# Transposing attention probabilities and keys by block transfers and VectorE instead of TensorE, in a hybrid decoder layer

## The chip, the cores and the metric

The kernel runs on one core of a Trainium2 chip. The metric is the device time of one execution in microseconds (us), as the median of several runs. Five engines matter here: TensorE (PE in the profile, its weight loads PEld), VectorE (DVE), ScalarE (ACT), GpSimd (POOL) and SyncE (SP), whose queue issues nearly all transfers. Each engine executes its own list of instructions in order and waits at semaphores for the others.

## The reference

One decoder layer on x of 2048 tokens by 1024 features, float32:

- RMSNorm, then one projection to 2816 columns that feeds two groups of heads.
- Four HGRN2 heads (128 wide): a gate f in (0, 1), k = 1 - f, state S_t = diag(f_t) S_{t-1} + k_t v_t^T, output S_t^T q_t, computed in chunks, then normed per head and multiplied by silu of a gate projection.
- Eight attention heads of 64 on two key/value heads, with a sliding window of 128 tokens and a learned sink logit per head that joins the softmax's denominator: each block of 128 queries sees its own and the previous block of 128 keys.
- Both groups together go through the output projection and are added to x; then RMSNorm, a gated MLP of 2816 with a causal depthwise convolution of three taps on the gate, a residual sum, and a last RMSNorm.

```python
p = jnp.exp(scores - m)
denom = jnp.sum(p, axis=-1, keepdims=True) + jnp.exp(sink - m)
out = jnp.einsum('bnhgqk,bnkhd->bnqhgd', p / denom, vb)
```

The sum over keys in the last line wants the probabilities with the keys on the partitions, while the softmax leaves them with the queries there. In the HGRN2 chunks, k v^T wants the keys' tokens on the partitions, while the projection leaves the features there. These are the two places where the kernel transposes and where the change is made.

## The kernel before, in words

Activations lie feature-major: a tile has 128 features on its partitions and 1024 tokens (HALF) in its rows. The sequence is worked in two halves, and each half runs through three stages: a mix stage (HGRN2 heads and attention), then the output projection with the gate/up products, then the down projection. Every float32 product of weights is three matmuls of a high and a low part (unit, L203 to L219).

In the mix stage (L1105 to L1127) the table ORDER names the pieces of four HGRN2 heads (hgrn: f, q, l, s, p) and four pairs of attention heads (attend: qa, sc, and twice pv or pw) in the order in which they are written. A scheduler with a timeline of its own then sets the final order of every engine's list, so that a change of an operation can shift instructions far away from it.

The pieces that the change touches:

- `sc` (L378 to L427): for each group g of four blocks of 128 queries, the scores are computed (psc, L399), copied to the tile sc, which holds 2 x 4 squares of 128 queries x 128 keys. A masked copy (L408) puts the own block's scores over the previous block's where the key is not after the query: as the window is as long as a block, each square holds every key once, the own block's in one triangle and the previous block's in the other. Then come the maximum (L411), eight exponentials on ACT (L421) and the division by the denominator (L426).
- `pv`, `pw` (L429 to L458): for each g, eight squares of sc are transposed by TensorE against the identity into PSUM (ppt, L435), VectorE multiplies each by two masks into po and pp (L438), and TensorE multiplies them with the values (poT, L446).
- `l` (L474 to L553): seven levels, m = 1 to 64. At each, TensorE makes plev (L517, L531) from K and Q, and VectorE multiplies K and Q by a factor (L523, L524, L534, L535) for the next level; plev is copied into ST by a masked copy (L542) or by ACT. The next level's matmuls wait for that level's Q or K.
- `s` (L555 to L579): K of the last level is transposed by TensorE in squares (pkn, L564), copied by ACT to Kn (L565) and multiplied with v (pu, L571).
- the carry (L345 to L347, L364 to L366): the last block of keys and values of the first half is kept for the second, by two VectorE copies each way.
- The output projection's first units are pop (L682, issued at L218); their operands XH and XL are splits of the finished heads (L225 to L234), and they stand partly among the last head's levels.

Weights come through `prep` (L192 to L201): a transfer on the SP queue into one of three raw tiles, an ACT cast and a VectorE difference.

Of the kernel before, what the change touches and what calls it, by code (L numbers as in the profile page):

```python
# [8 lines left out]
F32 = mybir.dt.float32  # L9
F32R = mybir.dt.float32r  # L10
U32 = mybir.dt.uint32
I32 = mybir.dt.int32
AF = mybir.ActivationFunctionType
ALU = mybir.AluOpType
# [3 lines left out]
P = 128  # L18
# [3 lines left out]
HALF = 1024  # L22
NH = S // HALF
TT = HALF // P
NB = HALF // 512
HG = 4
# [23 lines left out]
def hymba_layer(ctx: ExitStack, tc: tile.TileContext, a: dict, out: bass.AP, rows_out: bass.AP):  # L50
    nc = tc.nc
# [6 lines left out]
    cp = pool("const")  # L58
# [4 lines left out]
    dp = pool("dram", space=bass.MemoryType.DRAM)  # L63
# [5 lines left out]
    def ps(kind, name):  # L69
        return spaces[kind].tile([P, 512], F32, tag=kind, name=name)  # L70
# [6 lines left out]

    nmw = cp.tile([P, 16], F32, name="nmw")[:, 0:KT]
    nc.scalar.dma_start(nmw, a["norm_mix_w"])
    ones = cp.tile([P, P], F32, name="ones")  # L80
    nc.vector.memset(ones, 1.0)
    ident = cp.tile([P, P], F32, name="ident")
    state = cp.tile([P, HG, P], F32, name="state")
    warm = cp.tile([P, 32], F32, name="warm")[:, 0:1]
    nc.scalar.activation(warm, ones[:, 0:1], AF.Tanh)
    nc.gpsimd.memset(ident, 1.0)
    nc.gpsimd.affine_select(out=ident, in_=ident, compare_op=ALU.is_equal, fill=0.0,
                            base=0, pattern=[[-1, P]], channel_multiplier=1)
    halo = cp.tile([P, FT, 2], F32, name="halo")
    nc.vector.memset(halo, 0.0)  # L90
    kc = cp.tile([P, 2, P], F32R, name="kcarry")
    vc = cp.tile([P, P], F32, name="vcarry")

    class C:
        pass
# [3 lines left out]
    def constants():  # L99

        C.own = cp.tile([P, P], F32, name="own")
        C.ownT = cp.tile([P, P], F32, name="ownT")
        C.prevT = cp.tile([P, P], F32, name="prevT")
        for t, op, sgn in ((C.own, ALU.is_ge, 1), (C.ownT, ALU.is_ge, -1), (C.prevT, ALU.is_gt, 1)):
            nc.gpsimd.memset(t, 1.0)
            nc.gpsimd.affine_select(out=t, in_=t, compare_op=op, fill=0.0, base=0,
                                    pattern=[[-sgn, P]], channel_multiplier=sgn)

        C.lmask = {}
        for m in LEVELS[:5]:  # L110
            t = cp.tile([P, 2, 64], F32, name=f"lmask{m}")
            nb = 64 // m
            nc.gpsimd.memset(t, 1.0)
            for side in range(2):
                ts = t[:, side]
                nc.gpsimd.affine_select(out=ts, in_=ts, compare_op=ALU.is_ge, fill=0.0, base=-side * m,
                                        pattern=[[-2 * m, nb], [0, m]], channel_multiplier=1)
                nc.gpsimd.affine_select(out=ts, in_=ts, compare_op=ALU.is_ge, fill=0.0, base=m - 1 + side * m,
                                        pattern=[[2 * m, nb], [0, m]], channel_multiplier=-1)
            C.lmask[m] = t  # L120

        battn = C.battn = cp.tile([P, 6], F32, name="battn")
        nc.sync.dma_start(battn, a["b_attn"])
        C.bq = cp.tile([P, ATT_J], F32, name="bq")
        nc.vector.tensor_scalar(C.bq, battn[:, 0:ATT_J], 0.125, None, op0=ALU.mult)
        C.hgw = cp.tile([P, 1], F32, name="hgw")
        nc.sync.dma_start(C.hgw, a["hg_norm_w"])
        nc.vector.tensor_scalar(C.hgw, C.hgw, 0.5, None, op0=ALU.mult)
        C.sinkb = cp.tile([P, ATT_J, 2], F32, name="sinkb")
        nc.sync.dma_start(C.sinkb.rearrange("p j k -> p (j k)"), a["sinks"].to_broadcast([P, 8]))  # L130
        C.nfw = cp.tile([P, KT], F32, name="nfw")
        nc.sync.dma_start(C.nfw, a["norm_ffn_w"])
        C.fnw = cp.tile([P, KT], F32, name="fnw")
        nc.sync.dma_start(C.fnw, a["final_norm_w"])
        C.cw = cp.tile([P, FT, 4], F32, name="cw")
        nc.sync.dma_start(C.cw, a["conv"])

        lbl = cp.tile([P, 2, HG], F32, name="lbl")
        nc.sync.dma_start(lbl, a["lb_logits"])
        lbm = cp.tile([P, HG], F32, name="lbm")  # L140
        nc.vector.tensor_tensor(lbm, lbl[:, 0], lbl[:, 1], op=ALU.max)
        lbe = cp.tile([P, 2, HG], F32, name="lbe")
        nc.vector.tensor_tensor(lbe, lbl, lbm.unsqueeze(1).to_broadcast([P, 2, HG]), op=ALU.subtract)
        nc.scalar.activation(lbe, lbe, AF.Exp)
        nc.vector.tensor_tensor(lbm, lbe[:, 0], lbe[:, 1], op=ALU.add)
        nc.vector.reciprocal(lbm, lbm)
        C.lb = cp.tile([P, HG], F32, name="lb")
        nc.vector.tensor_tensor(C.lb, lbe[:, 0], lbm, op=ALU.mult)
        C.omlb = cp.tile([P, HG], F32, name="omlb")
        nc.vector.tensor_scalar(C.omlb, C.lb, -0.5, 0.5, op0=ALU.mult, op1=ALU.add)  # L150
        nc.vector.tensor_scalar(C.lb, C.lb, 0.5, 0.5, op0=ALU.mult, op1=ALU.add)
# [178 lines left out]
    def across(t, base, dims):  # L330

        v = t[:, :]
        return bass.AP(v.tensor, v.offset + base, [list(v.ap[0])] + dims)

    def rows(kv):
        return slice(kv * HD, (kv + 1) * HD)

    def att_keys(hf, kv, invb, p):
# [4 lines left out]
        KS = p.tile([P, 2, P + HALF], F32R, name="KS")  # L343
        V = p.tile([P, 1 + TT, P], F32, name="V")
        if hf:  # L345
            nc.vector.tensor_copy(KS[:, :, 0:P], kc)
            nc.vector.tensor_copy(V[:, 0], vc)  # L347
        kT, vT = [p.tile([P, HALF], F32, tag="f", name=n, bufs=2) for n in ("kT", "vT")]
        for jj, dst in ((ATT_J, kT), (ATT_J + 1, vT)):
            o = kv[jj - ATT_J]  # L350
# [11 lines left out]
                nc.tensor.transpose(pv[:, i * P:(i + 1) * P], vT[:, t0:t0 + P], ident)  # L362
            nc.scalar.copy(V[:, 1 + 4 * b:5 + 4 * b].rearrange("p a b -> p (a b)"), pv)
        if hf + 1 < NH:  # L364
            nc.vector.tensor_copy(kc, KS[:, :, HALF:HALF + P])
            nc.vector.tensor_copy(vc, V[:, TT])  # L366
        return KS, V

    def attend(hf, j, X, invb, KS, V, mix, p):
# [7 lines left out]
        yield  # L377
        scs = []  # L378
        for g in range(NB):
            sc = p.tile([P, 2, 4, P], F32, tag="sc", name="sc", bufs=2)  # L380
            gs = slice(g * 512, (g + 1) * 512)
            for kv in range(2):
                r, other = rows(kv), rows(1 - kv)
# [43 lines left out]
            scs.append(sc)  # L427
        yield
        for g, sc in enumerate(scs):  # L429
            pm = []  # L430
            for kv in range(2):
                pm.append([p.tile([P, 4, P], F32, tag="pp", name=n, bufs=4) for n in ("po", "pp")])
                pt = ps("at", "ppt")
                for i in range(4):
                    nc.tensor.transpose(pt[:, i * P:(i + 1) * P], sc[:, kv, i], ident)  # L435
                ptv = pt.rearrange("p (i q) -> p i q", i=4)
                for dst, mk in zip(pm[kv], (C.ownT, C.prevT)):
                    nc.vector.tensor_tensor(dst, ptv, mk.unsqueeze(1).to_broadcast([P, 4, P]), op=ALU.mult)  # L438
            oT = ps("at", "poT")
            for i in range(4):  # L440
                n = g * 4 + i
# [18 lines left out]
    def hgrn(hf, h, X, invb, vs, WG, gates, mix, p, fu=None):  # L460
# [95 lines left out]

        kept = TT if hf + 1 < NH else TT - 1
        Kn = p.tile([P, TT, P], F32, tag="t4", name="Kn", bufs=2)
        for b in range(NB):
            pk = ps("hg", "pkn")  # L560
            n = min(4, kept - 4 * b)
            for i in range(n):
                c = slice((b * 4 + i) * P, (b * 4 + i + 1) * P)
                nc.tensor.transpose(pk[:, i * P:(i + 1) * P], K[:, c], ident)  # L564
            nc.scalar.copy(Kn[:, 4 * b:4 * b + n].rearrange("p a b -> p (a b)"), pk[:, 0:n * P])  # L565
# [636 lines left out]
```

## Time and profile before

| | |
|---|---|
| median of 3 runs | 2150.81 us (2150.37 to 2150.9) |
| span of the profiled execution | 2149.0 us |
| the median above that span | 1.8 us |
| PE busy | 2130.8 us, 99% |
| PEld busy | 1790.6 us, 83% |
| DVE busy | 1632.2 us, 76% |
| ACT busy | 1020.2 us, 47% |
| transfers | 35.6% of 16 engines' span, 254.41 MB |

The page gives the span from the first to the last instruction of one execution; the runs' times lie 1.8 us above it. A busy share is an average over unlike stages. The mix stages lie at about 60 to 390 us and 1125 to 1450 us of the span, the gate/up and down stages between and after them. A matmul's row has a duration that is pipelined with the next one: what an instruction costs its engine is read from the distance between starts in the timeline, not from the duration.

### The profile page before, as it was taken

The page shows a single profiled execution, that of the slowest core. Times are in us where ns is not written, and L with a number is a line of the kernel's source. Part 1 is how long each engine was busy: PE and PEld are TensorE (multiplying, and loading weights), DVE is VectorE, ACT ScalarE, POOL GpSimd, SP SyncE. Part 2 cuts the span into 40 slices and gives each one's busy share as a digit, 9 for nine tenths or more (in the row PEclk, how much of TensorE's full clock was granted, in tenths as well). Part 3 has the DMA queues.
Part 4 walks back from the last instruction along what each step waited for, and adds up shares of the span by engine and source line. Part 5 has one row for each costly group of instructions (what it writes and reads, how often), then busy time and mean ns, then how long its engine had stood idle before and what let it go on. Part 6 is the DMA issues. An engine that isn't in the chain of part 4 may idle for free.

```text
span 2149.0 us, 29228 instructions
## 1 busy us (share of the span) xinstructions
PE 2130.8 (99%) x11271; PEld 1790.6 (83%) x11271; DVE 1632.2 (76%) x2443; ACT 1020.2 (47%) x1818; POOL 16.2 (1%) x45
## 2 busy tenths in 40 slices
PE   8999999999999999999999999999999999999998
PEld 6988988888888888888889889888888888888887
DVE  6576768788887888785775767677988888787765
ACT  5445554564444445345634446535544444443453
POOL 2000000000000000000000000000000000000000
PEclk9999999999999999999999999999999999999999
DMA  4111012413332334974641111124223323359743
GB/s 158 40 30 40 31 30 79 137 62 125 94 122 89 103 118 147 371 255 145 217 138 40 30 31 33 40 75 158 69 104 103 118 84 122 95 187 398 236 147 133
DMA packets 91147, 254.41 MB, mean 118 GB/s; under 512 B 11136, under 2 KB 13952, under 8 KB 91008
## 3 DMA queue, kind: packets, MB, share of 16 engines
q1 hardware_dynamic: 90576, 252.29, 35.3%
q8 instruction: 88, 1.44, 0.3%
q14 instruction: 51, 0.42, 0.1%
q10 hardware_dynamic: 432, 0.27, 0.0%
HBM read 195.37 MB, written 57.15 MB: 118 GB/s over the span
## 4 chain that ended last, share of the span: by engine, by line
PE 93%; DVE 5%; ACT 1%; issue 1%; DMA 0%; SPq 0%; DVEq 0%; ACTq 0%
PE X L767 7%; PE X L766 7%; PE X L765 7%; PE pop L218 6%; PE q L218 4%; PE f L218 4%; PE hq L218 4%; PE Y L767 4%; PE Y L765 4%; PE Y L766 4%; PE pdx L954 3%; PE pdx L953 3%; PE pdx L952 3%; PE g L218 3%; PE pdy L953 3%; PE pdy L954 3%
## 5 line engine op out<-in xcount | busy, mean ns | idle before, releaser
L638 ACT CAST whi<-raw 128x1024 fp32r<-128x1024 f32 x88 | 92.7, 1053 | 115.5 <-PE X L766 71.1
L765 PE MATMUL X<-T,whi 128*128 128x512 f32 x352 | 136.9, 389 | 0.0
L766 PE MATMUL X<-T,whi 128*128 128x512 f32 x352 | 136.9, 389 | 0.0
L767 PE MATMUL X<-T,wlo 128*128 128x512 f32 x352 | 136.9, 389 | 0.0
L836 DVE SCALAR_TENSOR_TENSOR y<-ga,cw,y 128x1024 f32<-128x1024 f32 x88 | 112.7, 1280 | 25.9 <-ACT y L834 25.8
L639 DVE TENSOR_TENSOR wlo<-raw,whi 128x1024 fp32r<-128x1024 f32 x88 | 107.3, 1219 | 4.4 <-ACT whi L638 4.4
L771 ACT COPY u<-X 128x512 f32<-128x512 f32 x88 | 51.6, 586 | 122.5 <-PE X L767 122.2
L199 ACT CAST whi<-raw 128x1024 fp32r<-128x1024 f32 x58 | 60.5, 1048 | 98.8 <-issue 20.6
L639 DVE TENSOR_TENSOR xld<-raw,xhd 128x1024 fp32r<-128x1024 f32 x72 | 81.1, 1132 | 17.8 <-ACT xhd L638 17.6
L638 ACT CAST xhd<-raw 128x1024 fp32r<-128x1024 f32 x72 | 69.8, 978 | 39.1 <-DMA raw<-act0T 14.0
L218 PE MATMUL pop<-XL,whi 128*128 128x512 f32 x256 | 84.2, 392 | 0.9 <-DVE XL L230 0.9
L218 PE MATMUL pop<-XH,wlo 128*128 128x512 f32 x256 | 83.3, 391 | 0.8 <-DVE wlo L200 0.8
L218 PE MATMUL pop<-XH,whi 128*128 128x512 f32 x256 | 83.1, 396 | 0.8 <-ACT XH L229 0.5
L200 DVE TENSOR_TENSOR wlo<-raw,whi 128x1024 fp32r<-128x1024 f32 x58 | 70.5, 1220 | 9.8 <-ACT whi L199 9.8
L767 PEld LDWEIGHTS X<-T,wlo 128*128 128x128 f32 x352 | 66.1, 188 | 13.7
L766 PEld LDWEIGHTS X<-T,whi 128*128 128x128 f32 x352 | 66.1, 188 | 13.7
L765 PEld LDWEIGHTS X<-T,whi 128*128 128x128 f32 x352 | 66.0, 188 | 13.7
L630 PE MATMUL pvv<-whi,XH 128*128 128x256 f32 x256 | 73.0, 286 | 0.0
L631 PE MATMUL pvv<-whi,XL 128*128 128x256 f32 x256 | 72.9, 286 | 0.0
L632 PE MATMUL pvv<-wlo,XH 128*128 128x256 f32 x256 | 71.9, 285 | 0.0
L767 PE MATMUL X<-B,wlo 128*128 128x512 f32 x176 | 68.7, 390 | 0.7 <-DVE wlo L639 0.7
L765 PE MATMUL X<-T,Sh 128*128 128x512 f32 x176 | 68.7, 390 | 0.0
(390 smaller groups left out, 6399.2 us busy)
## 6 DMA issues: line engine op xcount, KB each, us to landing
wr<-in_w_down SPq DMA_DIRECT2D x90, 512.0 KB, 5.6
raw<-in_w_gate SPq DMA_DIRECT2D x44, 512.0 KB, 3.6
raw<-in_w_up SPq DMA_DIRECT2D x44, 512.0 KB, 3.6
raw<-act0T SPq DMA_DIRECT2D x20, 512.0 KB, 5.9
raw<-act1T SPq DMA_DIRECT2D x20, 512.0 KB, 5.6
act0B<-y SPq DMA_DIRECT2D x33, 256.0 KB, 2.3
act1B<-y SPq DMA_DIRECT2D x33, 256.0 KB, 2.4
raw<-in_w_out SPq DMA_DIRECT2D x16, 512.0 KB, 3.7
```

The lines of the kernel that those rows point to most:

```text
L218: nc.tensor.matmul(o[b], w, x[:, bs], start=f, stop=l)
L630: nc.tensor.matmul(o[:, 0:256], xh[:, t], hi[:, c], start=kt == 0, stop=False)
L631: nc.tensor.matmul(o[:, 0:256], xl[:, t], hi[:, c], start=False, stop=False)
L632: nc.tensor.matmul(o[:, 0:256], xh[:, t], lo[:, c], start=False, stop=kt == KT - 1)
L638: nc.scalar.copy(h, src)
L639: return (eng or nc.vector).tensor_tensor(l, src, h.bitcast(F32), op=ALU.subtract)
L765: nc.tensor.matmul(o, wh[:, ws], xh, start=i == 0 and not more, stop=False, skip_group_check=more)
L766: nc.tensor.matmul(o, wh[:, ws], xl, start=False, stop=False, skip_group_check=more)
L767: nc.tensor.matmul(o, wl[:, ws], xh, start=False, stop=i == 3, skip_group_check=more)
L836: nc.vector.scalar_tensor_tensor(y, g[:, w:w + HALF], C.cw[:, ft, w:w + 1], y, op0=ALU.mult, op1=ALU.add)
L953: nc.tensor.matmul(o, wh[:, i, c], al[:, i, cols], start=False, stop=False, skip_group_check=more)
L954: nc.tensor.matmul(o, wl[:, i, c], ah[:, i, cols], start=False, stop=l, skip_group_check=more)
```

## The change

Four things change together.

- The eight squares of sc per group are no longer transposed by TensorE. A new helper `moved` issues 16 transfers on the SP queue; each takes a block of 32 partitions x 8 squares x 32 columns and puts it where the transposed square has that block, in runs of 32 floats (128 bytes). A second helper `turned` lets VectorE transpose every 32x32 block of the result in place of rows (one instruction for 128x1024). The results are md and pt, and they share the buffers of sc, of which there are now three instead of two.
- po is still pt times the mask ownT; pp is now pt minus po instead of pt times prevT.
- For heads 0 to 2, K is transposed to Kn by the same two helpers (over a tile Kd). Head 3 keeps TensorE's transposes.
- The carry goes through two small tiles in DRAM by four transfers; the tiles ones and prevT are gone.

```diff
-    kc = cp.tile([P, 2, P], F32R, name="kcarry")
-    vc = cp.tile([P, P], F32, name="vcarry")
+    kc = dp.tile([P, 2, P], F32, name="kcarry")
+    vc = dp.tile([P, P], F32, name="vcarry")
...
+    def moved(dst, src):
+
+        for a in range(4):
+            for c in range(4):
+                nc.sync.dma_start(dst[32 * c:32 * c + 32, :, 32 * a:32 * a + 32],
+                                  src[32 * a:32 * a + 32, :, 32 * c:32 * c + 32])
+
+    def turned(dst, src):
+
+        nc.vector.transpose(dst.rearrange("p a b -> p (a b)"), src.rearrange("p a b -> p (a b)"))
...
-            nc.vector.tensor_copy(KS[:, :, 0:P], kc)
-            nc.vector.tensor_copy(V[:, 0], vc)
+            nc.sync.dma_start(KS.bitcast(F32)[:, :, 0:P], kc)
+            nc.sync.dma_start(V[:, 0], vc)
...
-            sc = p.tile([P, 2, 4, P], F32, tag="sc", name="sc", bufs=2)
+            sc = p.tile([P, 2, 4, P], F32, tag="sc", name="sc", bufs=3)
...
         for g, sc in enumerate(scs):
+            md, pt = [p.tile([P, 8, P], F32, tag="sc", name=n, bufs=3) for n in ("md", "pt")]
+            moved(md, sc.rearrange("p a b c -> p (a b) c"))
+            turned(pt, md)
             pm = []
             for kv in range(2):
                 pm.append([p.tile([P, 4, P], F32, tag="pp", name=n, bufs=4) for n in ("po", "pp")])
-                pt = ps("at", "ppt")
-                for i in range(4):
-                    nc.tensor.transpose(pt[:, i * P:(i + 1) * P], sc[:, kv, i], ident)
-                ptv = pt.rearrange("p (i q) -> p i q", i=4)
-                for dst, mk in zip(pm[kv], (C.ownT, C.prevT)):
-                    nc.vector.tensor_tensor(dst, ptv, mk.unsqueeze(1).to_broadcast([P, 4, P]), op=ALU.mult)
+                ptv = pt[:, 4 * kv:4 * kv + 4]
+                own, prv = pm[kv]
+                nc.vector.tensor_tensor(own, ptv, C.ownT.unsqueeze(1).to_broadcast([P, 4, P]), op=ALU.mult)
+                nc.vector.tensor_tensor(prv, ptv, own, op=ALU.subtract)
...
         Kn = p.tile([P, TT, P], F32, tag="t4", name="Kn", bufs=2)
-        for b in range(NB):
+        if h < HG - 1:
+            Kd = p.tile([P, TT, P], F32, tag="SS", name="Kd", bufs=1)
+            moved(Kd, K.rearrange("p (c t) -> p c t", t=P))
+            turned(Kn, Kd)
+        for b in range(NB if h == HG - 1 else 0):
             pk = ps("hg", "pkn")
```

The scheduler makes a new order of the whole mix stage from this. Three places matter for what follows. The first is TensorE's list at the end of the first half's mix stage, in the levels of head 3 (pop is the output projection, ppt a transposed square, psc the scores, poT the product with the values). Before, around the matmuls of the level m = 4:

```order
L218 MATMUL pop_3548<-XH,wlo 128x512
L218 MATMUL pop_3549<-XH,wlo 128x512
L517 MATMUL plev<-Q,G 128x2x64 x4
L435 MATMUL ppt<-ident,sc 128x128 x4
L218 MATMUL pop_3623<-XH,whi 128x512
L218 MATMUL pop_3623<-XL,whi 128x512
```

And now, at the end of 24 pop matmuls:

```order
L216 MATMUL pop_3710<-XL,whi 128x512
L216 MATMUL pop_3710<-XH,wlo 128x512
L527 MATMUL plev<-Q,G 128x2x64 x16
L541 MATMUL plev<-Q,K 32x32 x16
L541 MATMUL plev<-Q,K 64x64 x8
L456 MATMUL poT<-po,V 64x128 x2
L578 MATMUL pkn<-ident,K 128x128 x8
L456 MATMUL poT<-pp,V 64x128 x2
```

Before, four matmuls of a level stand between long rows of pop (and of g and psc); now four levels (x16), the two coarse ones and pkn follow each other with two poT between. The pop matmuls that stood there are behind pu now. The second half's list has the same piece, with four psc after the level m = 2 and x12 after them.

The second place is VectorE's list beside it. Before, up to the factors of the level m = 2, for which the matmuls of m = 4 wait (XL is a split for the output projection, wlo a weight's low part, sc the masked copy of scores, hg the gate's product):

```order
L523 TENSOR_TENSOR K<-K,F_3003 128x2x128x2
L408 COPY_PREDICATED sc<-own,psc 128x256
L230 TENSOR_TENSOR XL<-hg_538,XH 128x1024
L230 TENSOR_TENSOR XL<-att_1697,XH 128x1024
L200 TENSOR_TENSOR wlo<-raw,whi 128x1024
L504 SCALAR_TENSOR_TENSOR hg_2104<-sg,hg_2104 128x512 x2
L230 TENSOR_TENSOR XL<-att_1508,XH 128x1024
L523 TENSOR_TENSOR K<-K,F_3015 128x2x64x4
L524 TENSOR_TENSOR Q<-Q,F_3003 128x2x128x2
```

Now, up to the same factors, and the later stretch in which the block transpose stands:

```order
L533 TENSOR_TENSOR K<-K,F_3071 128x2x128x2
L434 RECIPROCAL den<-den 128x8
L514 SCALAR_TENSOR_TENSOR hg_2139<-sg,hg_2139 128x512
L420 TENSOR_REDUCE m<-sc 128x8
L514 SCALAR_TENSOR_TENSOR hg_2139<-sg,hg_2139 128x512
L435 TENSOR_TENSOR sc<-sc,den 128x1024
L514 SCALAR_TENSOR_TENSOR hg_3033<-sg,hg_3033 128x512 x2
L533 TENSOR_TENSOR K<-K,F_3083 128x2x64x4
L423 TENSOR_TENSOR m<-m,sinkb 128x8
L534 TENSOR_TENSOR Q<-Q,F_3071 128x2x128x2
```

```order
L435 TENSOR_TENSOR sc<-sc,den 128x1024
L534 TENSOR_TENSOR Q<-Q,F_3107 128x2x16x16
L552 COPY_PREDICATED ST<-lmask_309,plev 128x2x16x16
L342 STREAM_TRANSPOSE pt<-md 128x1024
L544 TENSOR_TENSOR Q<-Q,F_3119 128x16x32
L545 TENSOR_TENSOR K<-K,F_3119 128x16x32
L447 TENSOR_TENSOR po<-pt,ownT 128x512
L448 TENSOR_TENSOR pp<-pt,po 128x512
L447 TENSOR_TENSOR po<-pt,ownT 128x512
L544 TENSOR_TENSOR Q<-Q,F_3141 128x8x64
L545 TENSOR_TENSOR K<-K,F_3141 128x8x64
```

The softmax of attention pair 3 stands among the levels now where splits and weight parts stood, and the block transpose and its masks stand ahead of the last two levels' factors.

The last place is the SP queue early in the first half. Before, weights alone stood there; now, in one piece (Kd and md are the targets of `moved`, 16 transfers each):

```order
L196 DMA raw<-in_w_f 128x1024
L374 DMA kcarry<-KS 256x1x128
L375 DMA vcarry<-V 128x128
L196 DMA raw<-in_w_g 128x1024
L196 DMA raw<-in_w_q 128x1024
L337 DMA Kd<-K 32x8x32 x16
L196 DMA raw<-in_w_att 128x1024 x2
L196 DMA raw<-in_w_g 128x1024
L337 DMA md<-sc 32x8x32 x16
L196 DMA raw<-in_w_f 128x1024
```

The transfers of blocks stand in the same queue as the weights, and a transfer that waits for its tile holds back the weights behind it.

More of the change, by code (lines that the diff above doesn't have):

```diff
@@ L79, in hymba_layer @@
     nc.scalar.dma_start(nmw, a["norm_mix_w"])
-    ones = cp.tile([P, P], F32, name="ones")
-    nc.vector.memset(ones, 1.0)
     ident = cp.tile([P, P], F32, name="ident")
@@ L84, in hymba_layer @@
     warm = cp.tile([P, 32], F32, name="warm")[:, 0:1]
-    nc.scalar.activation(warm, ones[:, 0:1], AF.Tanh)
+    nc.vector.memset(warm, 1.0)
+    nc.scalar.activation(warm, warm, AF.Tanh)
     nc.gpsimd.memset(ident, 1.0)
@@ L102, in constants @@
         C.ownT = cp.tile([P, P], F32, name="ownT")
-        C.prevT = cp.tile([P, P], F32, name="prevT")
-        for t, op, sgn in ((C.own, ALU.is_ge, 1), (C.ownT, ALU.is_ge, -1), (C.prevT, ALU.is_gt, 1)):
+        for t, op, sgn in ((C.own, ALU.is_ge, 1), (C.ownT, ALU.is_ge, -1)):
             nc.gpsimd.memset(t, 1.0)
@@ L364, in att_keys @@
         if hf + 1 < NH:
-            nc.vector.tensor_copy(kc, KS[:, :, HALF:HALF + P])
-            nc.vector.tensor_copy(vc, V[:, TT])
+            nc.sync.dma_start(kc, KS.bitcast(F32)[:, :, HALF:HALF + P])
+            nc.sync.dma_start(vc, V[:, TT])
         return KS, V
```

## The prediction

> **What bounds the kernel now.** I read the page first, then the busy time of single stretches, then the timelines at the places that the new order changes.
>
> ```profile
> span 2149.0 us, 29228 instructions
> PE 2130.8 (99%) x11271; PEld 1790.6 (83%) x11271; DVE 1632.2 (76%) x2443; ACT 1020.2 (47%) x1818; POOL 16.2 (1%) x45
> PEclk9999999999999999999999999999999999999999
> PE 93%; DVE 5%; ACT 1%; issue 1%; DMA 0%; SPq 0%; DVEq 0%; ACTq 0%
> ```
>
> TensorE works for 2130.8 of 2149.0 us, at full clock, and is 93% of the chain of waits: what leaves its list is won, as long as nothing makes it wait. VectorE's 76% is an average. The windows show its share at the end of the mix stages, where the change adds work to it (columns: stretch, length, PE, PEld, DVE, ACT, POOL, granted clock, DMA share, GB/s):
>
> ```profile
> core 0: us, PE busy (x) PEld busy (x) DVE busy (x) ACT busy (x) POOL busy (x), PEclk, DMA share, GB/s
> 320.00:340.00 20.00, 20.00 (x133) 16.97 (x132) 19.81 (x28) 11.47 (x19) 0.00 (x0) 1.00 0.49 154
> 340.00:372.00 32.00, 30.64 (x256) 25.29 (x256) 23.14 (x43) 12.35 (x45) 0.00 (x0) 1.00 0.13 37
> 1400.00:1430.00 30.00, 28.56 (x225) 23.34 (x226) 25.86 (x44) 9.45 (x29) 0.00 (x0) 1.00 0.28 96
> ```
>
> At 320 to 340 us both engines are full, 19.81 and 20.00 of 20: TensorE never waits although VectorE is saturated, because pop matmuls stand between the levels. In the two later stretches TensorE idles 32 - 30.64 = 1.4 and 30 - 28.56 = 1.4 us, 2.8 together.
>
> **What is removed.** All 128 transposes of probabilities go, and 45 of the 60 of keys (head 3 keeps 8 + 7): 173. Their price is the distance between starts, with the neighbours' own cost taken off (start, duration, instruction, count):
>
> ```profile
> L435 PE MATMUL ppt<-ident,sc 128*128 128x128 f32 x128 | 18.0, 273 | 0.0
> L564 PE MATMUL pkn<-ident,K x60: 270/272/301, 97.9 to 1427.0; 128*128 128x128 f32 x60
> 137.40 0.60 PE L435 MATMUL ppt<-ident,sc 128*128 128x128 f32 x4
> 137.76 0.70 PE L218 MATMUL q<-XH,wlo 128*128 128x512 f32 x2
> 138.29 0.63 PE L218 MATMUL q<-XH,whi 128*128 128x512 f32 x2
> 138.76 0.62 PE L218 MATMUL q<-XL,whi 128*128 128x512 f32 x2
> ```
>
> Two q take 138.76 - 138.29 = 0.47 us. The four transposes and two q before them take 138.29 - 137.40 = 0.89, so four transposes 0.42: 0.105 each. I take 0.11, so 173 x 0.11 = 19.0 us. The group's 18.0 busy us over 128 give 0.14 and 24.2 us as the upper end. [...]
>
> ACT loses twelve copies of pkn; nothing waits there, so I count them at zero, with TensorE's stream as cover. VectorE loses the four carry copies.
>
> **What is added.** VectorE gets 22 block transposes of 128x1024. No row shows one. The nearest rows are its other operations of that size (1.13 us, below); bounds are half and twice that, 0.6 to 2.3, and I take 1.13. The subtraction for pp costs what the product with prevT cost. SP gets 22 moves of 16 transfers and four carry transfers:
>
> ```profile
> 1.23 0.90 SPq L312 DMA_DIRECT2D x<-in_xP  x2
> 1390.53 0.33 SPq L198 DMA_DIRECT2D raw<-in_w_out  x1
> out<-h SPq DMA_DIRECT2D x12, 64.0 KB, 1.7
> ```
>
> Issued back to back a transfer costs 0.90 / 2 = 0.45 us of the queue, alone 0.33; the smallest frequent one lands after 1.7. A move is then 16 x 0.45 + 1.7 = 8.9 us; the ends are 7.0 (0.33 each) and 16.1 (0.9 each, twice the row, because one transfer is 256 runs of 128 bytes, which no row has). In the middle of the stage a move is covered: between a group's last exponentials and its poT stand rows of 512-column matmuls, 71 of them (16 us at 0.235) for the first pair. A weight queued behind a move is up to 8.9 us late; three raw tiles lie ahead of it, and I count nothing. The carry's reader stands a half later: nothing.
>
> **The order is what decides.** In the new lists the levels m = 2 to 16 of head 3, the two coarse levels and pkn follow each other with no pop between. TensorE then waits for VectorE's factors, so this stretch lasts as long as VectorE's list there. Prices on VectorE from these rows, start to start:
>
> ```profile
> 320.61 0.20 DVE L425 RECIPROCAL den<-den 128x8 f32<-128x8 f32 x1
> ...
> 327.50 1.32 DVE L542 COPY_PREDICATED ST<-lmask,plev 128x512 f32<-128x512 uint32 x1
> 328.61 1.26 DVE L230 TENSOR_TENSOR XL<-hg,XH 128x1024 fp32r<-128x1024 f32 x1
> ...
> 330.72 1.21 DVE L230 TENSOR_TENSOR XL<-hg,XH 128x1024 fp32r<-128x1024 f32 x1
> 331.86 1.21 DVE L230 TENSOR_TENSOR XL<-att,XH 128x1024 fp32r<-128x1024 f32 x1
> ...
> 345.01 0.70 DVE L542 COPY_PREDICATED ST<-lmask,plev 128x512 f32<-128x512 uint32 x1
> 345.61 0.68 DVE L504 SCALAR_TENSOR_TENSOR hg<-sg,hg 128x512 f32<-128x512 f32 x1
> 346.21 0.68 DVE L438 TENSOR_TENSOR po<-ppt,ownT 128x512 f32<-128x512 f32 x1
> ```
>
> 1.14 us for 1024 columns, 0.60 for 512, a masked copy 1.1 in the first levels and 0.60 later, 0.20 at most for 8 columns (0.12 taken; all at 0.20 would add 0.6). From the first factor (K by f, m = 1) to the last, K by F_3141, VectorE's list of the first half holds 22 operations of 512 columns (13.2 us), five masked copies (2 x 1.1 + 3 x 0.6 = 4.0), four of 1024 columns with the transpose (4.5), two masked copies of 256 columns (0.7) and seven small ones (0.8): 23.2 us.
>
> TensorE's work beside it, from its timeline:
>
> ```profile
> 339.27 1.05 PE L517 MATMUL plev<-Q,G 128*128 128x128 f32 x8
> 340.15 0.60 PE L435 MATMUL ppt<-ident,sc 128*128 128x128 f32 x4
> ...
> 351.85 0.70 PE L531 MATMUL plev<-Q,K 128*32 128x32 f32 x32
> ...
> 358.84 0.69 PE L531 MATMUL plev<-Q,K 128*64 128x64 f32 x16
> ```
>
> 24 pop at 0.235 (5.6), 8 psc (about 1.0), four levels at 340.15 - 339.27 = 0.88 (3.5), then the coarse levels' 0.70 and 0.69: 11.5 us. It waits 23.2 - 11.5 = 11.7, plus about 1 us that VectorE comes late behind pdiag: 13. In the second half VectorE's list holds 23.5 us, and den there waits for eight exponentials issued within the stretch:
>
> ```profile
> 121.38 0.39 ACT L421 ACTIVATE sc<-sc,m 128x128 f32<-128x128 f32 x1
> ...
> 124.62 0.19 ACT L421 ACTIVATION_READ_ACCUMULATOR sc<-sc,m 128x1 f32 x1
> ```
>
> They take 124.62 + 0.19 - 121.38 = 3.4 us, of which some 2.5 are not covered by the one factor, masked copy and small operations that stand ahead: 26, and about 27 with the late start, against 11 us of TensorE's work: 16. Together 29 us of waits where 2.8 stood: 26.
>
> Two smaller terms. In the second half pair 3's last block transpose stands nine operations of 512 columns (5.4 us) behind the division that its move waits for, and the move takes 8.9: VectorE stops 3.5 us, and the split XL of hg behind it, for which pop waits, is late by about 2.5. And the clock: after an idle start, TensorE ran slowly for some microseconds.
>
> ```profile
> 5.85 1.42 PE L218 MATMUL kv<-XH,whi 128*128 128x512 f32 x2 [5.85 <-ACT XH L232]
> 7.06 0.63 PE L218 MATMUL kv<-XL,whi 128*128 128x512 f32 x1
> 7.49 0.63 PE L218 MATMUL kv<-XH,wlo 128*128 128x512 f32 x1
> ```
>
> Starts 0.43 apart against 0.235 per q later. The waits in the new stretches are 2 to 3 us each with 0.9 us of work between. If the grant falls there, the levels' slower matmuls still lie inside the waits; the pop behind would run slowly for about 4 us, 2 us lost per half. Bounds 0 and 14 (all that stands there at half speed besides); I take 2. [...]
>
> **The sum.** -19.0 + 26 + 2.5 + 2 = +11.5: 2149.0 + 11.5 = 2160.5, and with the 1.8 us by which the runs' median lies above the span, about 2162.5. By the transpose at 0.14 it is 2157; by a block transpose of 0.6 or 2.3 us, one or two of which lie in each tail, some 1.5 us less or 4 more; by a clock term of 14, 2174. The forecast's own range is 2155 to 2175.
>
> **Rivals.** *Moves slower than their room* (slower, 2188). At 0.9 us per transfer a move takes 16.1. The first move of pair 3 has 10.6 us of VectorE's list ahead of its transpose in the tail, which it then exceeds by 5.5; the second one is 7.2 later than summed. Over two halves 2 x (5.5 + 7.2) = 25 more. It decides from about (10.6 - 1.7) / 16 = 0.56 us per transfer. For it: 256 runs of 128 bytes, and weights share the queue. Against it: the 0.33 of the lone transfers. [...]
>
> *The tails wait half as long* (faster, 2145 to 2146). If VectorE reaches the first factor with its splits and hg products already done, or its list runs beside TensorE's psc and pop better than summed, the extra waits come to some 13, with no late split (0) and a clock term of 0: -19 + 13 = -6, so 2145. It decides where the waits added are below 19. For it: 1.4 us of idle time was all that these stretches had before. Against it: at 320 to 340 us VectorE is already full, so it can't come early.
>
> *The wait is given back* (about 2152, no change). VectorE and the weights catch up while TensorE stands, and what idle time lies elsewhere (2149.0 - 2130.8 = 18.2, of which 5.9 lie ahead of the first matmul and 2.8 in the tails) shrinks by up to its remaining 9.5: 2162.5 - 9.5 = 2153. Against it: most of these waits are for the first inputs of a stage, not for a late engine.
>
> *A transpose costs TensorE its whole duration* (faster, 2134): 173 x 0.273 = 47 in place of 19. Against it: the starts above.
>
> **How the numbers follow.** Forecast 0.58, slow moves 0.19, half the waits 0.10, given back 0.11, the whole duration 0.02. The likeliest gives 2162.5. The range reaches from 2147, below the no-change case, to 2188, the slow moves. What a measurement can tell from no change is about 0.2%, 4.3 us: faster is below 2146.5, slower above 2155.1. Faster is half the waits and the whole duration, 0.12; no change is the given-back case, 0.11; slower is the rest, 0.77.
>
> **What would show it.** In the profile after: TensorE's busy time about 19 us lower; its idle time in the last 30 us of both mix stages about 14 each, put down to VectorE's Q and K (L534, L544, L545); the block transpose near 1.1 us; Kd and md transfers 0.45 apart on the queue; the clock dipping there or not. It is wrong if plev waits for less than half of that, if VectorE is seen idle ahead of the block transposes in the tails (then the moves decide), or if TensorE's waits lie in the middle of the mix stages, behind Kn, poT or weights, where I counted none.

## The result, and the profile after

| | before | after |
|---|---|---|
| median of the runs | 2150.59 us | 2172.88 us |
| ratio to before, 95% interval | | 1.0104 (1.009 to 1.0119) |
| span of the profiled execution | 2149.0 us | 2170.8 us |
| mean granted clock of TensorE | 0.999 | 0.988 |

The change makes the kernel 22.3 us slower. The forecast was 2162.5 us, 12 slower, with a range to 2188: sign and range hold, the size is half of what was measured. Two executions that took over three times as long as the others, 7016.05 us in the variant tail_two_queues and 7636.4 us in the kernel before, are left out of all times here. The page of the changed kernel (first rows, and the clock in 40 slices):

```profile
span 2170.8 us, 29356 instructions
PE 2128.5 (98%) x11098; PEld 1786.2 (82%) x11098; DVE 1655.6 (76%) x2461; ACT 1015.0 (47%) x1806; POOL 19.4 (1%) x43
PEclk9999998999999999999999999979999999999999
```

TensorE idles 2170.8 - 2128.5 = 42.3 us where it was 2149.0 - 2130.8 = 18.2: 24.1 more. And its busy time is only 2.3 us lower, although 173 instructions are gone. The slices with an 8 and a 7 in the clock's row are the ends of the two mix stages. The windows that were shown for the kernel before, and one more (stretch, length, PE, PEld, DVE, ACT, POOL, clock, DMA share, GB/s):

```profile
320.00:340.00 20.00, 17.99 (x130) 15.59 (x128) 18.52 (x33) 12.54 (x36) 0.00 (x0) 1.00 0.37 123
340.00:372.00 32.00, 22.93 (x162) 19.32 (x164) 24.15 (x44) 8.89 (x29) 0.00 (x0) 0.68 0.26 50
1400.00:1430.00 30.00, 19.29 (x165) 16.81 (x163) 26.93 (x49) 15.03 (x52) 0.00 (x0) 0.72 0.18 40
1430.00:1460.00 30.00, 25.55 (x164) 21.57 (x165) 11.72 (x29) 6.39 (x22) 0.00 (x0) 0.82 0.18 42
```

Nearly all of the loss stands here: TensorE is idle for 26.2 us of these 112, and the granted clock is down to 0.68. What TensorE waits for is read in its timeline, first half (start, duration, instruction, count, idle ahead of it and what ended it), with one row of the second half at the end:

```profile
336.92 1.07 PE L527 MATMUL plev<-Q,G 128*128 128x128 f32 x8
342.50 2.04 PE L527 MATMUL plev<-Q,G 128*128 128x128 f32 x8 [4.51 <-ACT G L525]
345.42 2.04 PE L527 MATMUL plev<-Q,G 128*128 128x128 f32 x8 [0.88 <-DVE Q L534]
348.34 2.05 PE L527 MATMUL plev<-Q,G 128*128 128x128 f32 x8 [0.87 <-DVE Q L534]
351.17 1.07 PE L541 MATMUL plev<-Q,K 128*32 128x32 f32 x32 [0.78 <-DVE Q L534]
354.95 1.12 PE L541 MATMUL plev<-Q,K 128*64 128x64 f32 x16 [2.71 <-DVE K L545]
...
358.08 1.94 PE L578 MATMUL pkn<-ident,K 128*128 128x128 f32 x8 [0.60 <-DVE K L545]
...
1414.00 2.04 PE L527 MATMUL plev<-Q,G 128*128 128x128 f32 x8 [3.04 <-ACT G L525]
```

The levels of head 3 wait for VectorE's Q and K, and for G, ACT's copy of that K. After the first long wait the same eight matmuls take 2.04 us instead of 1.07. The granted clock there is half of full speed in three stretches (the third one follows a wait of 2.94 us for the split XL):

```profile
341.40:361.90 20.50, 12.84 (x102) 11.05 (x104) 15.02 (x26) 7.17 (x25) 0.00 (x0) 0.50 0.25 41
1413.20:1437.10 23.90, 13.94 (x112) 12.22 (x113) 16.19 (x28) 7.38 (x26) 0.00 (x0) 0.50 0.25 42
1443.90:1447.40 3.50, 3.50 (x10) 2.73 (x9) 2.89 (x8) 0.00 (x0) 0.00 (x0) 0.51 0.56 206
```

TensorE works for 12.84 + 13.94 + 3.50 = 30.3 us at half clock, so an estimated 15.1 us of its busy time are due to the clock. Without them its work is 2.3 + 15.1 = 17.4 us less than before. The span's growth is then complete: 24.1 more idle + 15.1 - 17.4 = 21.8 us. The rows of VectorE beside it, some of the factors and a block transpose:

```profile
331.89 0.69 DVE L533 TENSOR_TENSOR K<-K,f 128x512 f32<-128x512 f32 x1
344.58 0.69 DVE L534 TENSOR_TENSOR Q<-Q,F 128x512 f32<-128x512 f32 x1 [0.40 <-PE plev L527]
347.50 0.69 DVE L534 TENSOR_TENSOR Q<-Q,F 128x512 f32<-128x512 f32 x1 [0.79 <-PE plev L527]
352.39 1.25 DVE L342 STREAM_TRANSPOSE pt<-md 128x1024 f32<-128x1024 f32 x1 [0.65 <-issue]
357.26 0.68 DVE L545 TENSOR_TENSOR K<-K,F 128x512 f32<-128x512 f32 x1
```

From the first factor to the last, 357.94 - 331.89 = 26.1 us pass. VectorE now also waits for TensorE: its factor changes Q in place and must let the slow plev read Q first (0.40, 0.79). In the kernel before, the same stretch was not shorter but longer, and TensorE had more pop to do in it:

```profile
323.56 0.69 DVE L523 TENSOR_TENSOR K<-K,f 128x512 f32<-128x512 f32 x1
360.19 0.69 DVE L535 TENSOR_TENSOR K<-K,F 128x512 f32<-128x512 f32 x1
```

That is 360.88 - 323.56 = 37.3 us. The pop matmuls ahead of head 3's pkn, before and now, are counted in windows over the tile pop that end there (stretch, length, PE, PEld and DVE of pop alone, clock, DMA share, GB/s):

```profile
320.00:361.00 41.00, 19.46 (x78) 14.18 (x78) 0.00 (x0) 1.00 0.34 103
320.00:358.00 38.00, 11.43 (x48) 8.76 (x48) 0.00 (x0) 0.78 0.31 83
```

It is the same in the second half, 78 and 48. The other 30 (30 x 0.23 = 6.9 us) stand behind pu now.

### The profile page after: what moved, and what is told of

Same layout as the page of the kernel before. It is cut to its first block, busy times and chain, and to the rows that moved or that the text cites. A ratio compares the mean times of both kernels' runs of the same rounds, so it can differ in the third digit from the quotient of the medians.

```text
span 2170.8 us, 29356 instructions
## 1 busy us (share of the span) xinstructions
PE 2128.5 (98%) x11098; PEld 1786.2 (82%) x11098; DVE 1655.6 (76%) x2461; ACT 1015.0 (47%) x1806; POOL 19.4 (1%) x43
## 4 chain that ended last, share of the span: by engine, by line
PE 93%; DVE 4%; SPq 1%; ACT 1%; DMA 1%; issue 0%; DVEq 0%; ACTq 0%
PE X L781 7%; PE X L780 7%; PE X L779 7%; PE pop L216 7%; PE hq L216 4%; PE g L216 4%; PE f L216 4%; PE q L216 4%; PE Y L781 4%; PE Y L780 4%; PE Y L779 4%; PE pdx L967 3%; PE pdx L966 3%; PE pdx L968 3%; PE pdy L967 3%; PE pdy L966 3%
## 5 line engine op out<-in xcount | busy, mean ns | idle before, releaser
L652 ACT CAST xhd<-raw 128x1024 fp32r<-128x1024 f32 x72 | 69.6, 977 | 39.6 <-DMA raw<-act1T 13.6
L779 PE MATMUL Z<-B,whi 128*128 128x512 f32 x176 | 68.7, 390 | 0.0
```

What stands on the lines that cost most here:

```text
L652: nc.scalar.copy(h, src)
L779: nc.tensor.matmul(o, wh[:, ws], xh, start=i == 0 and not more, stop=False, skip_group_check=more)
```

## The experiments

The theory after this profile: the ends of the mix stages last as long as VectorE's list, the waits let the clock fall, and the fallen clock adds to both. The rivals: the missing pop between the levels; the block transfers in their queue; and, for the size of the gain, that a transpose is worth less than 0.11 us. Ratios are to the kernel before as it ran beside each variant (medians of 2150.07 to 2150.30 us).

**One part alone: the probabilities.**

```diff
-        if h < HG - 1:
+        if False:
             Kd = p.tile([P, TT, P], F32, tag="SS", name="Kd", bufs=1)
...
-        for b in range(NB if h == HG - 1 else 0):
+        for b in range(NB):
```

> Only the probabilities go by block transfers; the keys of all heads stay on TensorE. 45 transposes come back (45 x 0.11 = 5 us). All moves of the last stretch of the mix stages stay, but the scheduler's order now has 24 and more pop between the levels and the coarse levels of head 3. If the row of levels without pop costs the time: TensorE's idle time in the last 60 us of both mix stages together falls from 27 to about 10, the granted clock stays near 1.00 there, and the time is 2172.9 + 5 - 17 - 14 = 2147, within 2140 to 2158. If the transfers cost it (0.61 us each on the queue): 16 of 22 moves are left, the ones in the tails among them, and the time stays above 2165.

Measured 2165.29 us, 1.0067 (1.0051 to 1.0084), clock 0.994. It is 7.6 us faster than the whole change, and 18 slower than the theory said, just above the 2165 from which the expectation saw the transfers as the cause. The order had its pop back, 76 ahead of pkn in each half: the missing pop cannot be the whole cause.

**The other part alone: the keys.** Probabilities as before, heads 0 to 2 with Kd, Kn and the block transpose; the carry as in the change.

> Only the keys of heads 0 to 2 go by block transfers; the probabilities stay on TensorE. 45 transposes leave TensorE, nothing is added to the last stretch, and pop stands between the levels as in the kernel before. If a transpose is worth 0.11 us and moves in the middle of the stage are covered: 2150.6 - 5 = 2146, within 2142 to 2150. If moves hold back the weights in the queue or the split of the state: 2152 or more.

Measured 2154.55 us, 1.0021 (1.0012 to 1.003), clock 0.999. No clock is lost and no move stands in the tails; still TensorE idles 6.4 us more than before (span 2153.3 less 2128.7 busy = 24.6), at the ends of the mix stages. Even this part does not pay; alone the two cost 15.0 and 4.2 us against the kernel before beside them, together 22.3.

**Only the order: pop held back.**

```diff
+HOLD = {0: {0: 1, 1: 1, 2: 2, 3: 2, 4: 4, 5: 4}, 1: {0: 8, 1: 8, 2: 8, 3: 16, 4: 16, 5: 16}}
...
             for i, kt in enumerate(order):
...
+                with tc.issue_after(marks[hold[i]].ins) if i in hold else ExitStack():
```

> All operations of the changed kernel; only TensorE's order differs: the first six operands of the first two output units are held behind the levels of head 3, so that some 16 us of pop instead of 5.6 stand between the level m = 1 and the coarse levels. If the waits and the fallen clock of these rows are the cause: idle time in the last 60 us of both mix stages falls from 27 to some 10, the clock stays near 1.00, and the time is 2172.9 - 17 - 12 = 2144, within 2136 to 2154. If the moves (11.6 us each) are the cause: nothing of them changes, 2165 or more.

Measured 2168.74 us, 1.0086 (1.0071 to 1.0101), clock 0.993: 4 us of the 29 expected. TensorE's timeline in the first half shows why:

```profile
323.16 1.25 PE L621 MATMUL pot<-ident,on 128*128 128x128 f32 x8 [1.89 <-DVE on L616]
...
342.24 1.68 PE L529 MATMUL plev<-Q,G 128*128 128x128 f32 x8 [4.49 <-ACT G L527]
...
358.18 1.94 PE L580 MATMUL pkn<-ident,K 128*128 128x128 f32 x8 [0.60 <-DVE K L547]
```

In the first half the pop that were put between the levels are missing ahead of them: TensorE came to them earlier, waited for VectorE there (1.89 us ahead of pot), and pkn starts at 358.18 as it did at 358.08. In the second half more pop stand ahead of pkn than the changed kernel's 48:

```profile
320.00:358.10 38.10, 13.38 (x48) 9.51 (x48) 0.00 (x0) 0.93 0.31 87
1393.00:1441.00 48.00, 20.02 (x76) 14.88 (x76) 0.00 (x0) 0.82 0.35 93
```

The first half's last pop stands 0.5 us later than in the changed kernel and the second half's 4.6 us earlier, so the 4 us were won where more pop stood ahead of pkn. Moving the 48 about won nothing. To bring the other 30 forward in both halves, with VectorE's list as it is, was not tried.

**The clock: a filler.** Twelve matmuls that nobody reads ahead of each level of head 3 from m = 2 on. The same edit holds two operands of the first two pop units behind pu, so that 48 pop stay ahead of pkn as in the changed kernel.

```diff
             pl = ps("hg", "plev")
+            for u in range(FILL if h == HG - 1 and m > 1 else 0):
+                nc.tensor.matmul(pl[:, u % 4 * P:u % 4 * P + P], ident, ident, start=True, stop=True)
```

> The changed kernel, with twelve matmuls of the identity with itself (1.3 us) ahead of each level of head 3 from m = 2 on; nothing reads them. TensorE has 16 us more to do over both halves, all of it where it waits for VectorE's factors; the pop stay in the stretch where they stood. If the clock falls because of these waits and the slow levels hold up VectorE's next factor: clock 1.00, and the time falls by 8 to 14 us, to about 2161. If the waits alone cost the time and the clock is a side effect: 2173 or a few us more.

Measured 2165.51 us, 1.0071 (1.0056 to 1.0086), clock 0.999.

```profile
344.57 2.84 PE L525 MATMUL plev<-ident 128*128 128x128 f32 x24
347.25 1.06 PE L532 MATMUL plev<-Q,G 128*128 128x128 f32 x8
```

A level is back at 1.06 us. The filler takes 347.25 - 344.57 = 2.7 us, twice what I had reckoned; twelve such fillers per execution are 32 us of useless work, and the kernel is 7.4 us faster with it. That the clock falls because TensorE waits, and that the fall costs time, is shown.

> The filler again, six matmuls per level instead of twelve. The twelve took 2.67 us by their starts, longer than VectorE needs per level (2.3), so TensorE itself set the pace of the levels at 3.6 us; six take 1.3 us. If the loss was waits plus the fallen clock: the clock stays at 1.00, the levels go at VectorE's 2.3 to 2.5 us, and the time is 2165.5 - 12 = about 2154. If six are too few to hold the clock: clock 0.99 as in the changed kernel, 2166 to 2173.

Six matmuls per level: 2162.05 us, 1.0057 (1.0041 to 1.0074), clock 0.998. With a shorter filler 3.5 us more come back, not the 12 expected: TensorE now waits again in the first half's levels, 1.80 us for G, 0.49 for Q and 2.39 for K. So about 11 us of the change's loss can be had back by keeping the clock up, and 11 remain.

**What the removed work is worth.** The kernel before, without the 173 transposes and with nothing in their place (VectorE reads sc and ACT reads K as they lie; the output is another one).

```diff
-                pt = ps("at", "ppt")
-                for i in range(4):
-                    nc.tensor.transpose(pt[:, i * P:(i + 1) * P], sc[:, kv, i], ident)
-                ptv = pt.rearrange("p (i q) -> p i q", i=4)
+                ptv = sc[:, kv]
```

> The kernel before, with the 173 transposes left out and nothing put in their place: VectorE's masks read the probabilities as they lie in sc, and the keys of heads 0 to 2 are copied to Kn untransposed, so the output is another one. It gives the price of what the change removes. If a transpose is worth its 0.11 us wherever it stands: 2150.6 - 19 = 2132, within 2128 to 2137. If the last stretch of the mix stages is bound by VectorE's list (10.0 of 10 us busy at 330 to 350 us of the kernel before), the transposes there and whatever else lets TensorE arrive earlier win nothing: 2138 to 2148.

Measured 2147.38 us, 0.9988 (0.9979 to 0.9998): 3.2 us less than 2150.59 for all 173, 2.8 less than the kernel before beside it. Its page, its tail, and a wait of each engine there:

```profile
PE 2120.0 (99%) x11098; PEld 1778.6 (83%) x11098; DVE 1630.5 (76%) x2443; ACT 1021.6 (48%) x1818; POOL 20.5 (1%) x45
...
340.00:372.00 32.00, 25.83 (x200) 22.21 (x199) 17.83 (x42) 10.62 (x42) 0.00 (x0) 0.89 0.06 18
...
347.05 0.17 DVE L424 TENSOR_TENSOR den<-den,es 128x8 f32<-128x8 f32 x1 [2.40 <-ACT sc L421]
353.71 0.70 PE L443 MATMUL poT<-pp,V 128*64 128x128 f32 x4 [2.32 <-DVE pp L435]
```

TensorE's busy time falls by 10.8 us, although 8.8 of the busy microseconds in the tails are at half clock (5.59 at 352.5 to 359.3 and 3.17 at 1424.3 to 1427.7); counted at full speed 10.8 + 4.4 = 15.2 us are removed. Of these 8.2 come back as idle time, which rises from 18.2 to 2146.4 - 2120.0 = 26.4, and 4.4 as half clock. TensorE waits in the tail mostly for VectorE's results. VectorE isn't full there (17.83 of 32 us): it waits itself, among others for the exponentials of pair 3. So TensorE, with less work in hand, meets a chain of results over VectorE and ACT; the order is also another one. Most of the gain that the change aims at is gone before any of its own costs come in.

**Pair 3 on TensorE.** The pair that stands among the levels keeps its transposes; the other moves stay.

```diff
+            if j < ATT_J - 1:
...
+            else:
+                # as in the kernel before: ppt, then po and pp
```

> The changed kernel, but attention pair 3 of each half, the one that stands among the levels of head 3, keeps TensorE's transposes (32, 3.4 us); four moves and four block transposes (4 x 1.2 us of VectorE) leave the tails. If the tail's length is VectorE's list and the moves ahead of it: 4.8 us less of VectorE's time, no wait for a move in the tails, 26 pop between the coarse levels, clock near 1.00, about 2154. If only the missing pop between the first levels matter: they are missing still, 2166 or more.

Measured 2159.31 us, 1.0043 (1.0028 to 1.0058), clock 0.995: 13.6 us of 22.3 back, 5 less than expected. Ahead of pkn stand 78 pop again. Here the work among the levels is cheaper on TensorE, the engine that waits there.

**What the transfers cost.** First left out (the block transpose reads sc and K where they lie, so that only the blocks are turned), then issued and landing but read by nobody.

```diff
-            moved(md, sc.rearrange("p a b c -> p (a b) c"))
-            turned(pt, md)
+            turned(pt, sc.rearrange("p a b c -> p (a b) c"))
```

> The changed kernel with the 352 block transfers left out: the block transpose reads sc and K where they lie, so only the blocks are turned, not their places, and the output is another one. VectorE's list keeps its 22 block transposes. If the transfers cost the time (VectorE stands 31 us at its block transposes waiting for them): 2140 or less. If VectorE's own list in the tails and the clock cost it: 2155 to 2168.

> The changed kernel with all 352 block transfers issued and landing in md and Kd, but nobody reads them: the block transpose reads sc and K where they lie, as in the kernel without transfers, so the output is another one. The order is near that of the kernel without transfers (pop between the levels of head 3). If the transfers cost the time by making what stands behind them late (VectorE's block transposes, and the order that the scheduler makes of that): 2151.5 to 2156. If they cost it in the queue, ahead of the weights, or by the bandwidth they take: 2162 or more.

(The second one keeps the lines with moved.) Measured 2151.48 us, 1.0008 (0.9999 to 1.0018), and 2151.90 us, 1.0007 (0.9998 to 1.0017). So issuing and landing 352 transfers, in the queue ahead of the weights, costs 0.4 us, nothing that can be told apart. That VectorE reads what they bring costs 2172.9 - 2151.9 = 21.0. Two things change with that: VectorE's waiting, and the order. With unread transfers 78 pop stand ahead of pkn in each half instead of 48, and only 2060 of VectorE's 2461 instructions stand in a common order. The waiting in the changed kernel (waits of VectorE: total, times, longest; then the issues of one queue and their landing):

```profile
DVE pt L342 <- DMA md<-sc: 28.4, 10, 9.2
L337 SPq DMA_DIRECT2D md<-sc x256: 585/609/1857, 124.0 to 1437.7; - x128
md<-sc SPq DMA_DIRECT2D x256, 32.0 KB, 1.9
```

With unread transfers the first row is 8.4 us in 5 times, not zero; md and pt share the buffers of sc there too. A transfer takes 0.61 us of the queue and lands after 1.9: 16 x 0.61 + 1.9 = 11.7 us a move. Of the 28.4 us 25.2 lie in the middle of the stages, where TensorE hardly waits, and I had taken them for free. They are not clearly so. In the 270 us from the first half's first pdiag on, the changed kernel (first row) has VectorE busy for 4.8 us less than the one with unread transfers, while TensorE is as busy in both:

```profile
60.50:330.50 270.00, 269.88 (x1923) 236.65 (x1922) 190.99 (x358) 131.18 (x345) 1.57 (x3) 1.00 0.26 64
60.60:330.60 270.00, 269.78 (x1928) 236.97 (x1928) 195.74 (x368) 136.69 (x363) 1.57 (x3) 1.00 0.24 56
```

So VectorE comes late to the end of the stage; in the second half it is 3.6 us by the same count. That its waits for md are the reason is likely, not shown, as the order differs.

**Are the moves in the tails too slow?** Every second transfer of pair 3 goes on ACT's queue.

```diff
-            moved(md, sc.rearrange("p a b c -> p (a b) c"))
+            moved(md, sc.rearrange("p a b c -> p (a b) c"), (nc.sync, nc.scalar if j == ATT_J - 1 else nc.sync))
```

> The changed kernel, with every second transfer of attention pair 3's moves issued on ACT's queue instead of SP's; TensorE's and VectorE's lists stay the same up to the last factor of head 3 but for a few neighbours that change places. A move in the tails then takes some 7 us instead of 11.6. If the lateness of these four moves decides (waits of 0.7 and 1.0 us for md in the first half, 0.5 and 1.8 in the second, and pop's 2.9 us for XL behind it): about 5 us less, 2168. If VectorE's own list decides: within 2 us of 2172.9.

Measured 2170.0 us, the median of 2169.6, 2170.0 and 2171.55, 1.0094 (1.0078 to 1.0111): 2.9 us less, between the two values of the expectation. The lists are nearly the changed kernel's (2448 of VectorE's 2461 instructions stand in a common order). The lateness of these four moves is a small part.

> The same for all 22 moves. VectorE's 28 us of standing at block transposes for md falls by more than half, and the weights wait less in SP's queue. The scheduler gives another order, with pop between some levels. If the transfers' 21 us (2172.9 against 2151.5 without them) come from moves that are late for VectorE, all over the stage: 2160 or less. If ACT, which would issue 176 transfers, is held up by them (0.6 us each would be 106 us): 2175 or more.

All moves on both queues: 2195.8 us, 1.0212 (1.0196 to 1.0227). This is the second guess of the expectation.

```profile
60.00:300.00 240.00, 230.48 (x1638) 201.50 (x1637) 155.12 (x287) 103.65 (x289) 1.04 (x2) 0.98 0.24 53
L337 ACTq DMA_DIRECT2D md<-sc x128: 592/622/1279, 127.5 to 1466.7; - x128
```

An issue holds ACT's queue for 0.62 us. ACT's copies of poT (att) wait 13.0 us for these transfers, in two waits. TensorE now idles 9.5 us in the middle of the first mix stage, where it had idled 0.1.

**Less work for VectorE: splits on GpSimd.**

```diff
-                    M[n] = split(mix[n])
+                    M[n] = split(mix[n], eng=nc.gpsimd)
```

> The changed kernel, but the low parts of the six splits XL ahead of the output projection in each half (1.13 us each on VectorE, 6.8 us in the last 60 us of a half) are made by GpSimd, which is idle. If VectorE's list sets the end of the mix stages: up to 6.8 us less per half and less of the fallen clock, 2172.9 - 10 to - 20, about 2158. If GpSimd takes much longer for one than 1.13 us (no run shows it yet) and pop waits for XL, or the order without pop is what costs: 2170 or more.

Measured 2182.66 us, 1.0151 (1.0134 to 1.0168): 10 slower. The rows of GpSimd and of VectorE say why:

```profile
311.99 2.42 POOL L228 TENSOR_TENSOR XL<-att,XH 128x1024 fp32r<-128x1024 f32 x1 [2.16 <-ACT XH L227]
314.37 4.74 POOL L228 TENSOR_TENSOR XL<-hg,XH 128x1024 fp32r<-128x1024 f32 x2
...
312.15 2.28 DVE L179 TENSOR_TENSOR t<-y 128x8 f32<-128x8 f32 x1
314.46 2.33 DVE L180 TENSOR_TENSOR t<-t,ms 128x8 f32<-128x8 f32 x1
...
323.76 0.17 DVE L181 SCALAR_TENSOR_TENSOR y<-t,y 128x8 f32<-128x8 f32 x1
```

While GpSimd works at its 2.4 us each, VectorE's operations of 8 columns take 2.3 instead of 0.17. VectorE's busy time rose from 1655.6 to 1667.3 us, although 12 operations left it, so this run doesn't test the theory; it shows another way to make VectorE late, and the time followed.

No variant of the change beats the kernel before; the only faster kernel, without transposes, leaves out what it must compute.

## Why the prediction came out as it did

The sum of the prediction can be laid beside the trace, term by term: -19.0, 26 + 2.5 and 2 were forecast; work removed -17.4, idle time added 24.1 and half clock 15.1 were measured. The forecast work is 1.6 us too much, the forecast waits are 4.4 us too long, and the forecast clock term is 13.1 too small. (The forecast's last step, 2149.0 + 11.5 + 1.8, is 2162.3 and not 2162.5.)

*"173 x 0.11 us = 19.0 us".* As work removed this is near: 17.4 us, 0.10 each. The price isn't settled to better than a factor of two: without transposes it is 15.2 us, 0.09 each, and in keys_alone, where no clock was lost, 2.1 us of busy time for 45, 0.05 each. But what it wins in time is 3.2 us, with nothing put in its place. The step that failed is the one ahead of the sum, that what leaves TensorE's list is won "as long as nothing makes it wait": in the tails the removal itself makes it wait and lets the clock fall. The 1.4 us of idle time in each tail, which I quoted, did not tell how soon that begins. In the sum it didn't show, because the same waits were counted under the next term.

*"The order is what decides", 26 us of waits.* The size is about right: 24.1 us more idle time in all, the late split's wait among it. VectorE's list took 26.1 us in the first half where I had 23.2, and 1431.34 - 1404.59 = 26.8 in the second where I had 27. The reason that I gave, that no pop stands between the levels, is in part right: 30 pop of 78 have gone from ahead of pkn, and held_pop won its 4 us in the half in which they were back. It isn't all: att_alone has 76 there in both halves and still loses 15 us. VectorE also comes later: its first factor of head 3 stands at 331.89 instead of 323.56. That VectorE's list became longer between the first and the last factor is not the cause, for it was 37.3 us before. How much of the waits is VectorE's lateness and how much the missing pop stays open, since no run changed one of them alone.

*The late split XL, 2.5 us.* Measured in the second half:

```profile
1442.62 0.73 PE L216 MATMUL pop<-XL,whi 128*128 128x512 f32 x2 [2.94 <-DVE XL L228]
```

*The clock, 2 us between bounds of 0 and 14.* This is the term that was mis-sized, and it is more than the 10 us between forecast and result: 15.1 by the busy time at half clock, some 11 by the filler. Even the upper bound of 14 was a little low. I argued that the levels' slower matmuls lie inside the waits. They don't all: the next factor writes Q in place and waits for them (0.40, 0.79 us), so plev at half speed delays VectorE too; and the coarse levels, pkn and poT run slowly as well. My waits of 2 to 3 us were also an average; the longest were 4.51 and, in the second half, 3.75. That pop would run slowly for some 4 us per half, on which the 2 rests, was my estimate from the slow start (starts 0.43 us apart up to 9.62), where the granted clock is recorded as 1.00. The runs show in its place 12.84 and 13.94 us of work at half clock in the two tails, and 3.50 us of it among pop, in the second half. In both halves the clock falls in the first long wait: 3.4 us into the one of 4.51 us, and 2.2 us into the one of 3.04.

*The moves: 0.45 us per transfer, covered in the middle.* Measured 0.61 and 1.9, so 11.7 us instead of 8.9; that is just past the point (0.56) from which the rival of slow moves was to decide. That rival's place was wrong: with every second transfer of the tails' moves on another queue 2.9 us come back, while reading moved data over the whole stage, with the order that comes with it, costs 21. Of the prediction's signs of being wrong one is there in part: VectorE stands idle ahead of the tails' block transposes, 0.65, 1.01, 0.46 and 1.77 us. *"I count nothing"* for weights behind a move was right, by the kernel that doesn't read them.

*The block transpose at 1.13 us* has a duration of 1.24, and its starts lie 1.2 from the next; a small miss. The rivals on the faster side didn't occur: no wait was halved or given back.

The parts as the runs give them: without transposes -3.2, with VectorE's block transposes in place of them (and the carry and the third buffer) +4.1, with the transfers unread +0.4, with VectorE reading what they bring +21.0; sum +22.3, of which some 11 come back with the clock held up. What stays open is how the 21 divide into VectorE's standing for the moves and the order that the scheduler makes of them: every change of a move changed the order too, save the one that showed 2.9 us.

## What to carry to other kernels

An engine that is 99% busy is not the bound of each stretch: look for the windows in which a second engine is full as well, or in which the first one already waits a little for it. There the first one's work may be worth little, and the question is what keeps its waits filled. A wait in the middle of a stage that costs TensorE nothing may still cost, if it delays an engine that TensorE meets at the stage's end. And here the granted clock fell to 0.50 in waits of 4.51 and 3.04 us, and the eight matmuls of a level then took 2.04 us instead of 1.07: where such waits are expected, price the matmuls behind them at that speed too, on the path wherever another engine waits for them.

## What the runs showed of the hardware that was not expected

- Useless work made the kernel faster: 32 us of matmuls with no reader took it from 2172.9 to 2165.5, six in place of twelve per level to 2162.1.
- A matmul of the identity with itself, 128x128 in f32, takes 2.68 / 12 = 0.22 us by its starts and is two instructions in the trace, while a transpose of the same size takes 0.105 by the prediction's rows and is one.
- The granted clock fell 341.4 - 338.0 = 3.4 us after the first long wait began, but 1413.2 - 1411.0 = 2.2 us after that of the second half began, and once more at 1443.9, when TensorE had been at work again for 1.3 us after a wait of 2.94.
- In splits_on_pool VectorE's operations of 8 columns went from 0.17 to 2.3 us while GpSimd ran operations of 1024 columns (2.4 us). Those of 2.28 and 2.33 us at 312.15 and 314.46 end at 314.43 and 316.79; GpSimd's end at 314.41 and, for the first of the two in the row at 314.37, at an estimated 316.74 (half of the row's 4.74 us). The last of GpSimd's ends at 319.07 + 4.62 = 323.69, and VectorE's next operation of 8 columns, at 323.76, takes 0.17 again.
- A transfer of 256 runs of 128 bytes holds its queue for 0.61 us against 0.33 for a lone transfer of whole rows, on SP as on ACT (0.62).
